# The FFN of a hybrid block: 16 of the 22 inner tiles of the down projection by seven block products, and a bank of its own for the fourth product of the up projection

## The chip, the core and the metric

One core of a Trainium2 chip runs the whole block. TensorE (PE) multiplies, VectorE (DVE), ScalarE (ACT) and GpSimd (POOL) do elementwise work, SyncE (SP) issues the DMAs; each engine works through its instructions in the order in which they were issued, and semaphores tie the engines together. The metric is the device time of one launch, in microseconds. A profiled execution is one further launch.

## The reference, cut to what matters

Sequence 1024, D_MODEL 1024, D_FF 2816, all in float32. The three mixers before the FFN are not touched.

```python
h = rms_norm(x, pre_ffn_norm[l])
u = causal_dwconv(h @ ffn_w_up[l], ffn_conv_w[l], ffn_conv_b[l])   # 1024 x 5632, three taps
gate, val = jnp.split(u, 2, axis=-1)
f = (jax.nn.gelu(gate, approximate=True) * val) @ ffn_w_down[l]    # 2816 -> 1024
x = x + rms_norm(f, post_ffn_norm[l])
```

## The kernel before

Everything is held transposed, features on partitions and tokens along the row, so a tile is 128 features by 512 tokens, and h (0 or 1) names the half of the sequence. Each float32 product is made of three matmuls on operands split into a high and a low part: hi·hi, hi·lo, lo·hi, each 128x128 by 128x512 (all recorded at line L208). ACT makes the high part by a copy into the matmul type; DVE or POOL makes the low part, a subtraction with two inputs in SBUF.

The 2816 inner features are 22 tiles f. Tile f has a gate tile (2f) and a value tile (2f+1) in the up projection.

*Up projection.* The first four f go directly (`up_half`, L1530). The other 18 go through `up_pair` (L1537). It regards gate and value for the two halves of the sequence as a 2x2 block matrix and makes it by seven block products instead of eight. A block product is four steps of 128 inner features with three matmuls each, so 12 matmuls, and one pair costs 84. `weights7` (L500) loads the two weight tiles (`wraw`, three buffers in rotation) and makes the seven weight operands: `whi`/`wlo` (products 1 and 2), `uf` with `uhi`/`ulo` twice (products 3, 6 and 5, 7), `ahi`/`alo` (product 4). ACT makes the high parts, POOL the sums `uf` and the low parts: per pair eight operations at L512 to L526. The activations' combinations are made once, ahead of the loop (L1571 to L1589).

In `up_pair` three PSUM banks x, y, z take the products; a `snap` (L1510) is ACT's copy of a bank into SBUF. Products 1, 6, 5 and 3 accumulate in x, product 2 goes to y, products 7 and 4 accumulate in z. DVE adds the first snap to y (L1545) and takes the second from z (L1557); POOL takes the third from the snap of z (L1555). `conv` applies the three taps: ACT writes the first, DVE adds two (L310), and for h = 1 two short operations add the halo of two columns that h = 0 left (L312). For h = 1 the value tile's conv reads the snap s7, in SBUF. ACT applies gelu (L1524), DVE multiplies gate by value (`gated`, L1527), and SP stores the tile m to `m_d` in DRAM.

*Down projection.* It goes over the inner tiles in chunks, `DOWN`: (first tile, count) = (0,4), (4,4), (8,4), (12,4), (16,2) and, in the tail with the norm, (18,4). `m_split` (L1598) reloads m, ACT makes the high part (L1601), DVE the low part (L1602). `down` (L1608) goes over the eight output tiles j: it loads and splits a weight tile (`load_w`, L267: ACT L272, POOL L273), runs 12 matmuls per tile of four inner tiles for each half, and adds the bank to the accumulator `acc[h][j]` in SBUF (L1617; for the first chunk ACT copies it, L1615). The first chunk's reload stands inside the last up pair (`between`), and all loads are issued by SP in program order; buffers come free when the matmuls that read them are done. What stands after (18,4), the norm and the residual, is the tail, L1634 on.

The banks named `dense` rotate in one pool, `psd`; the tail has another, `psn`.

Of the kernel before, what the change touches and what calls it, by code (L numbers as in the profile page):

```python
# [23 lines left out]
NFF = 22  # L24
# [68 lines left out]
def layout(a):  # L93
# [31 lines left out]
    for i, (c0, c1) in enumerate(TM_CHUNKS):  # L125
# [16 lines left out]

    dns = [units(dn[c * 128:(c + n) * 128], ar(DM)) for c, n in DOWN]
    out.update(
# [9 lines left out]
        wup=units(up, fch), **{f"wdn{i}": d for i, d in enumerate(dns)})  # L154
# [4 lines left out]
DOWN = [(0, 4), (4, 4), (8, 4), (12, 4), (16, 2), (18, 4)]  # L159
# [25 lines left out]
U_BUFS = 4  # L185
OSQ = 6

# [1169 lines left out]
def tail_stage(nc, tc, es, env):  # L1357
# [152 lines left out]
    def snap(ps):  # L1510
        s = up_.tile([128, 512], F32, name="snap", bufs=5)
        act(s, ps, AF.Copy)
# [24 lines left out]
    def up_pair(f, rhs, between=None):  # L1537

        st = {}
        w = E.weights7(wx, A["wup"][2 * f], A["wup"][2 * f + 1], 512)  # L1540
        x, y, z = bank(), bank(), bank()
        E.product(x, w, rhs, 1, True)
        s1 = snap(x)
        E.product(y, w, rhs, 2, True)
        V.tensor_tensor(y, y, s1, op=OP.add)  # L1545
        conv(2 * f, 0, y, st)
        E.product(x, w, rhs, 6, False)
        s2 = snap(x)
# [6 lines left out]
        P.tensor_tensor(s7, s7, s3, op=OP.subtract)  # L1555
        E.product(z, w, rhs, 4, False)
        V.tensor_tensor(z, z, s2, op=OP.subtract)  # L1557
# [14 lines left out]
    later = []  # L1572
    for k in range(4):
        quarters = [(1, h2[0, k]), (2, h2[0, k + 4]), (3, h2[1, k + 4])]
        lows = [rows[0][k], rows[1][k], rows[0][k + 4], rows[1][k + 4]]
        E.combos(*lows, V)
        for q, b in quarters:
            rhs[q][k] = b
        t2, t1, t4, t3 = lows
        for q, t in ((6, t2), (7, t3)):  # L1580
            rhs[q][k] = hi, lo = x_t(), x_t()
            act(hi, t, AF.Copy)
            V.tensor_tensor(lo, t, fl(hi), op=OP.subtract)
        later += [(5, k, t1, hi_t), (4, k, t4, lo_t)]

    for q, k, t, place in sorted(later, key=lambda x: (-x[0], x[1])):
        rhs[q][k] = hi, lo = place(), x_t()
        act(hi, t, AF.Copy)
        V.tensor_tensor(lo, t, fl(hi), op=OP.subtract)  # L1589
# [3 lines left out]
    def m_tile(f, h, s):  # L1593
        t = x_t(F32) if s is None else up_.tile([128, 512], F32, name=f"u{s}")
        nc.sync.dma_start(t, m_d[f * 128:(f + 1) * 128, hs(h)])
        return t

    def m_split(f, h):  # L1598
        src = m_tile(f, h, None if f < DOWN[0][1] else f % 2)
        hi, lo = hi_t(), lo_t()  # L1600
        act(hi, src, AF.Copy)  # L1601
        V.tensor_tensor(lo, src, fl(hi), op=OP.subtract)  # L1602
        return hi, lo
# [4 lines left out]
    def down(ci, f0, nf, ms):  # L1608
        end = None
        for j in range(8):  # L1610
            pss = fm_unit(psd, load_w(A[f"wdn{ci}"][j], nf * 128), lambda k, h: ms[f0 + k, h], nf)
            for h, ps in enumerate(pss):
                a = acc[h][j]
                if ci == 0:
                    act(a, ps, AF.Copy)  # L1615
                else:
                    end = V.tensor_tensor(a, a, ps, op=OP.add)  # L1617
        return end


    ms0 = {}
    for f in range(N_FIRST, NFF):
        up_pair(f, rhs, (lambda: ms0.update(m_chunk(*DOWN[0]))) if f == NFF - 1 else None)

    last = len(DOWN) - 1
    tc.keep_in_program_order(nc.scalar.preload_act_table_set(E.TABLE))
    for ci, (f0, nf) in enumerate(DOWN[:last]):
        if ci == 0:
            acc = [[x_t(F32) for _ in range(8)] for _ in range(2)]
        i = down(ci, f0, nf, m_chunk(f0, nf) if ci else ms0)  # L1630
        if ci == last - 2:
            late = i
# [5 lines left out]
    def w_split(j, place):  # L1638
        ws.append(load_w(A[f"wdn{last}"][j], 512, place, up_.tile([128, 512], F32, name="snap", bufs=5)))
# [17 lines left out]
    def norm_rows(ss, W):  # L1657
# [7 lines left out]
        rb = up_.tile([128, 512], F32, name="u1")  # L1665
# [15 lines left out]
    for s0, s1 in LAST:  # L1681
# [3 lines left out]
        ss = up_.tile([128, 512], F32, name="u0")  # L1685
        for j in range(8):
# [10 lines left out]
            else:  # L1697
                sq = up_.tile([128, 512], F32, name="snap", bufs=5)
# [24 lines left out]
```

## Time and profile before

| what | us |
| --- | --- |
| three runs | 2288.7, 2292.17, 2292.13 |
| their median | 2292.13 |
| the profiled execution | 2297.28 |
| its span | 2295.5 |
| mean granted clock of PE | 0.985 |
| first block product after the last wait at its start | 1699.38 |
| end of the wait at the border of up and down projection | 2011.85 |

In the profile a row of a group names line, engine, operation, output and inputs with their shapes, the count, the busy time and the mean of one, and behind the bar the idle time of the engine just before these instructions and what ended it. A row of the waits gives the engine that waited, what it waited for, and the sum in us, how often and the longest. In a timeline a row gives the start, the duration, and in brackets the idle time before. The clock is the share of the full rate that was granted to PE.

### The profile page before, as it was taken

To read this page: it belongs to the slowest core of one execution; us is meant where nothing else is said; L and a number is where in the kernel's file an instruction comes from. 1 tells how busy PE (TensorE), PEld (TensorE's weight loads), DVE (VectorE), ACT (ScalarE), POOL (GpSimd) and SP (SyncE) were. 2 spreads that over 40 slices of the span, in tenths; PEclk is the share of its full clock that TensorE was granted. 3 is DMA by queue.
4 is the path that set the end of the run, shared out by engine and by line. 5 is a ranking of instruction groups with operands and counts; after the bars stand their busy time and mean duration, and the time that the engine had idled before them with its cause. 6 is when DMAs were issued, how large, how long until landed. Compare 5 with 4: busy or idle time off the path is not lost.

```text
span 2295.5 us, 29758 instructions
## 1 busy us (share of the span) xinstructions
PE 2197.3 (96%) x10663; PEld 1755.3 (76%) x10663; DVE 1346.2 (59%) x2376; ACT 1164.9 (51%) x2185; POOL 1184.5 (52%) x853
## 2 busy tenths in 40 slices
PE   7999999998999999999999999999899999999997
PEld 7878889865665678878775678887678888878886
DVE  7765554268567526556536653359876777744346
ACT  6544443466756646667755421245545555553124
POOL 3676741246736733333347655446578888822213
PEclk9999999999999999999999999999999999999998
DMA  4233341320221011112253253334322222264212
GB/s 170 81 111 108 116 132 62 112 70 24 62 67 31 12 56 42 60 65 93 83 211 112 80 213 129 119 128 162 106 79 86 85 83 83 84 223 130 93 32 74
DMA packets 115349, 222.03 MB, mean 97 GB/s; under 512 B 28160, under 2 KB 42432, under 8 KB 115200
## 3 DMA queue, kind: packets, MB, share of 16 engines
q1 hardware_dynamic: 112608, 217.80, 28.0%
q10 hardware_dynamic: 2592, 2.32, 0.3%
q8 instruction: 84, 1.38, 0.2%
q14 instruction: 65, 0.53, 0.1%
HBM read 162.80 MB, written 57.28 MB: 96 GB/s over the span
## 4 chain that ended last, share of the span: by engine, by line
PE 77%; DVE 11%; ACT 5%; issue 3%; DMA 3%; POOL 2%; SPq 0%; DVEq 0%; ACTq 0%; POOLq 0%
PE dense L208 55%; PE ps_s L208 7%; PE ps_o L208 6%; PE ps_t L208 6%; PE ps_b L208 4%; POOL wlo L273 1%; DVE x L1484 1%; DVE mx L938 1%; DVE u L310 1%; DVE osq L1457 1%; DVE x L1589 1%; DMA wraw<-in_wdn 1%; DMA wraw<-in_wfm 0%; DVE x L1677 0%; DMA x<-in_xT 0%
## 5 line engine op out<-in xcount | busy, mean ns | idle before, releaser
L273 POOL TENSOR_TENSOR wlo<-wraw,whi 128x1024 fp32r<-128x1024 f32 (+2 forms) x134 | 266.5, 1989 | 444.1 <-ACT whi L272 435.4
L208 PE MATMUL dense<-hi,whi 128*128 128x512 f32 x816 | 308.2, 392 | 4.8 <-ACT whi L272 4.8
L208 PE MATMUL dense<-hi,wlo 128*128 128x512 f32 x752 | 289.3, 394 | 8.9 <-POOL wlo L273 7.9
L208 PE MATMUL dense<-lo,whi 128*128 128x512 f32 x688 | 269.3, 392 | 0.5 <-POOL lo L1497 0.5
L208 PE MATMUL dense<-h_hi,whi 128*128 128x512 f32 x656 | 263.8, 402 | 0.0
L208 PE MATMUL dense<-h_lo,whi 128*128 128x512 f32 x656 | 257.5, 393 | 0.0
L208 PE MATMUL dense<-h_hi,wlo 128*128 128x512 f32 x656 | 257.2, 392 | 0.0
L272 ACT ACTIVATE whi<-wraw 128x1024 fp32r<-128x1024 f32 (+2 forms) x134 | 116.1, 867 | 277.4 <-PE dense L208 228.8
L976 POOL TENSOR_TENSOR wT_lo<-wT,wT_hi 128x512 fp32r<-128x512 f32 x132 | 168.5, 1288 | 101.3 <-ACT wT_hi L975 93.2
L208 PEld LDWEIGHTS dense<-hi,whi 128*128 128x128 f32 x816 | 154.2, 189 | 39.5 <-ACT whi L272 6.9
L208 PE MATMUL dense<-x,uhi 128*128 128x512 f32 x552 | 177.3, 392 | 3.9 <-ACT x L584 2.4
L208 PEld LDWEIGHTS dense<-hi,wlo 128*128 128x128 f32 x752 | 142.1, 189 | 41.7 <-POOL wlo L273 10.4
L208 PEld LDWEIGHTS dense<-lo,whi 128*128 128x128 f32 x688 | 130.0, 189 | 28.6 <-POOL lo L1497 1.4
L208 PEld LDWEIGHTS dense<-h_hi,wlo 128*128 128x128 f32 x656 | 123.7, 189 | 26.7
L208 PEld LDWEIGHTS dense<-h_hi,whi 128*128 128x128 f32 x656 | 124.4, 190 | 23.8
L208 PEld LDWEIGHTS dense<-h_lo,whi 128*128 128x128 f32 x656 | 124.3, 189 | 22.5
L1180 POOL TENSOR_TENSOR s_lo<-sa,s_hi 128x512 fp32r<-128x512 f32 (+2 forms) x48 | 53.5, 1115 | 152.1 <-ACT s_hi L1179 152.1
L938 DVE TENSOR_REDUCE mx<-ps_t 128x1 f32<-128x384 f32 (+3 forms) x192 | 98.7, 520 | 47.7 <-PE ps_t L208 44.0
L208 PEld LDWEIGHTS dense<-x,uhi 128*128 128x128 f32 x552 | 103.7, 189 | 27.5 <-ACT x L584 3.6
L965 ACT ACTIVATE wT<-ps_s 128x512 f32<-128x512 f32 x132 | 78.4, 594 | 72.4 <-PE ps_s L208 67.1
L310 DVE SCALAR_TENSOR_TENSOR u<-dense,pv,u 128x510 f32<-128x510 f32 (+1 forms) x140 | 101.9, 737 | 7.8 <-ACT u L306 7.6
L521 POOL TENSOR_TENSOR ulo<-uf,uhi 128x1024 fp32r<-128x1024 f32 x30 | 72.5, 2418 | 63.4 <-ACT uhi L520 63.4
(514 smaller groups left out, 5690.9 us busy)
## 6 DMA issues: line engine op xcount, KB each, us to landing
wraw<-in_wfm SPq DMA_DIRECT2D x62, 512.0 KB, 3.7
wraw<-in_wup SPq DMA_DIRECT2D x52, 512.0 KB, 3.7
g_d<-gate_e SPq DMA_DIRECT2D x48, 256.0 KB, 2.1
s_d<-o SPq DMA_DIRECT2D x48, 256.0 KB, 2.0
ge<-g_d SPq DMA_DIRECT2D x24, 512.0 KB, 3.5
m_d<-u SPq DMA_DIRECT2D x44, 256.0 KB, 2.0
u<-m_d SPq DMA_DIRECT2D x36, 256.0 KB, 4.0
row<-s_d SPq DMA_DIRECT2D x16, 512.0 KB, 4.2
```

Of the source, the lines that this page charges most:

```text
L208: i = f(*a, **k)
L272: act(hi, raw, AF.Copy)
L273: (V if tiles else P).tensor_tensor(lo, raw, fl(hi), op=OP.subtract)
L310: V.scalar_tensor_tensor(o[:, d:], ps[:, :512 - d], taps[d], o[:, d:], op0=OP.mult, op1=OP.add)
L521: P.tensor_tensor(l24, f24, fl(h24), op=OP.subtract)
L938: V.tensor_reduce(mx[:, h, a, n:n + 1], pm[:, :w], axis=AX, op=OP.max)
L965: act(w.rearrange("p h q -> p (h q)"), pz, AF.Exp)
L976: P.tensor_tensor(lo, wf, fl(hi), op=OP.subtract)
L1180: (P if SB_SLO else V).tensor_tensor(s_lo[:, c0:], a[:, c0:], fl(s_hi[:, c0:]), op=OP.subtract)
L1457: eng.tensor_tensor(sums[0], sums[0], sq, op=OP.add)
L1484: e.tensor_tensor(o[j], o[j], x, op=OP.add)
L1589: V.tensor_tensor(lo, t, fl(hi), op=OP.subtract)
```

## The change

Down projection: the inner tiles 4 to 19 go in four chunks of four (`DOWN7`) through `down7`. In a chunk the four inner tiles make two 2x2 block matrices of m (two inner tiles by the two halves of the sequence), k = 0 and 1; an output block takes two steps of 128, and there are two halves d of the output (four tiles each). Each half d takes one `weights7` call on weights stored in the matching order (`wds`), and seven block products for n = 0 and 1, each 2 x 3 matmuls: 84 matmuls for a half, 672 for all. Each product is added to, or taken from, one accumulator tile as its bank is done: 14 evictions for a half. The remaining tiles go as before, (20,2) by `down` and (0,4) in the tail.

The combinations of m are made in the up loop: for every two inner tiles `combine` makes four DVE operations on SBUF tiles, deferred into the following pair, and SP issues 14 stores of a 128x512 tile to a new scratch `m7_d`, where it issued four to `m_d`. `m_sets` reloads them, 14 tiles for a chunk, each with a copy by ACT and a split by DVE; the load goes straight into the tile of the low part. The first chunk's loads stand in the last up pair, as before; chunk c's loads stand in the program ahead of chunk c's products.

Up projection: the fourth product gets a bank v from the pool `psn`. The snap of z and POOL's subtraction go. DVE takes the second snap's place by `s2 = z - s2`, then `v += s2` and `z -= s3`; the conv of h = 1 for the value tile reads the bank z.

Buffers: gate tiles `u0` 6, value tiles `u1` 2, snaps 6 (before: four, four and five).

```diff
-DOWN = [(0, 4), (4, 4), (8, 4), (12, 4), (16, 2), (18, 4)]
+DOWN7 = [4, 8, 12, 16]
+DOWN = [(20, 2), (0, 4)]
...
+U0_BUFS = 6
+U1_BUFS = 2
+SNAPS = 6
 OSQ = 6
...
     m_d = E.scratch("m_d", [NFF * 128, T])
+    m7_d = E.scratch("m7_d", [4 * len(DOWN7) // 2 * 7 * 128, 512])
 
     def conv(u, h, ps, st):
         s = u % 2
         if h == 0:
             st["halo", s] = up_.tile([128, 4], F32, name="halo", bufs=12)
-        st[s, h] = up_.tile([128, 512], F32, name=f"u{s}")
+        st[s, h] = up_.tile([128, 512], F32, name=f"u{s}", bufs=(U0_BUFS, U1_BUFS)[s])
         E.conv(st[s, h], h, ps, [pvc(PV_FW, 3 * u + 2 - d) for d in range(3)], pvc(PV_FB, u), st["halo", s])
         if s == 0:
             act(st[0, h], st[0, h], AF.Gelu_apprx_tanh)
 
+    even = {}
+    def in_pairs(f):
+        return DOWN7[0] <= f < DOWN7[-1] + 4
+    def m7_rows(p, q):
+        r = (7 * p + q - 1) * 128
+        return m7_d[r:r + 128, :]
     def gated(f, h, st):
-        V.tensor_tensor(st[0, h], st[0, h], st[1, h], op=OP.mult)
-        nc.sync.dma_start(m_d[f * 128:(f + 1) * 128, hs(h)], st[0, h])
+        m = st[0, h]
+        V.tensor_tensor(m, m, st[1, h], op=OP.mult)
+        if not in_pairs(f):
+            nc.sync.dma_start(m_d[f * 128:(f + 1) * 128, hs(h)], m)
+            return
+        if f % 2 == 0:
+            even[h] = m
+            q = {0: 1}.get(h)
+        else:
+            q = 2 + h
+        p = (f - DOWN7[0]) // 2
+        if q:
+            nc.sync.dma_start(m7_rows(p, q), m)
+        if f % 2 and h:
+            later.extend(combine(p, even[0], even[1], st[0, 0], m))
+    later = []
+    def combine(p, b11, b12, b21, b22):
+        t7, t6, t4 = [up_.tile([128, 512], F32, name="snap", bufs=SNAPS) for _ in range(3)]
+        def one():
+            V.tensor_tensor(t7, b12, b22, op=OP.subtract)
+            V.tensor_tensor(b12, b11, b12, op=OP.subtract)
+            for q, t in ((7, t7), (5, b12)):
+                nc.sync.dma_start(m7_rows(p, q), t)
+        def two():
+            V.tensor_tensor(t6, t7, b11, op=OP.subtract)
+            V.tensor_tensor(t4, t6, b21, op=OP.add)
+            for q, t in ((6, t6), (4, t4)):
+                nc.sync.dma_start(m7_rows(p, q), t)
+        return one, two
+    def deferred():
+        if later:
+            later.pop(0)()
 
...
         st = {}
         w = E.weights7(wx, A["wup"][2 * f], A["wup"][2 * f + 1], 512)
         x, y, z = bank(), bank(), bank()
+        v = psn.tile([128, 512], F32, name="psn", tag="psn")
         E.product(x, w, rhs, 1, True)
         s1 = snap(x)
         E.product(y, w, rhs, 2, True)
         V.tensor_tensor(y, y, s1, op=OP.add)
         conv(2 * f, 0, y, st)
+        deferred()
         E.product(x, w, rhs, 6, False)
         s2 = snap(x)
         if between:
             between()
         E.product(z, w, rhs, 7, True)
-        s7 = snap(z)
+        V.tensor_tensor(s2, z, s2, op=OP.subtract)
         E.product(x, w, rhs, 5, False)
         s3 = snap(x)
-        P.tensor_tensor(s7, s7, s3, op=OP.subtract)
-        E.product(z, w, rhs, 4, False)
-        V.tensor_tensor(z, z, s2, op=OP.subtract)
-        conv(2 * f + 1, 0, z, st)
+        E.product(v, w, rhs, 4, True)
+        V.tensor_tensor(v, v, s2, op=OP.add)
+        conv(2 * f + 1, 0, v, st)
+        V.tensor_tensor(z, z, s3, op=OP.subtract)
         gated(f, 0, st)
+        deferred()
         E.product(x, w, rhs, 3, False)
-        conv(2 * f + 1, 1, s7, st)
+        conv(2 * f + 1, 1, z, st)
         conv(2 * f, 1, x, st)
         gated(f, 1, st)
 
...
-    def m_tile(f, h, s):
-        t = x_t(F32) if s is None else up_.tile([128, 512], F32, name=f"u{s}")
-        nc.sync.dma_start(t, m_d[f * 128:(f + 1) * 128, hs(h)])
-        return t
+    def split_in(src):
+        hi, lo = hi_t(), lo_t()
+        return split_to(hi, lo, src)
+    def split_to(hi, lo, src):
+        nc.sync.dma_start(fl(lo), src)
+        act(hi, fl(lo), AF.Copy)
+        V.tensor_tensor(lo, fl(lo), fl(hi), op=OP.subtract)
+        return hi, lo
 
     def m_split(f, h):
-        src = m_tile(f, h, None if f < DOWN[0][1] else f % 2)
-        hi, lo = hi_t(), lo_t()
-        act(hi, src, AF.Copy)
-        V.tensor_tensor(lo, src, fl(hi), op=OP.subtract)
-        return hi, lo
+        return split_in(m_d[f * 128:(f + 1) * 128, hs(h)])
+    def m_sets(c):
+        sets = [{}, {}]
+        for n, q in enumerate(ORDER7):
+            for i, st in enumerate(sets):
+                if (2 * c + i) % 3 == 2 and n < 5:
+                    hi, lo = x_t(), x_t()
+                else:
+                    hi, lo = hi_t(), lo_t()
+                st[q] = split_to(hi, lo, m7_rows(2 * c + i, q))
+        return sets
+    def down7(c, sets):
+        def product2(ps, q, n, first):
+            hi, lo = w[q]
+            for k in range(2):
+                s = slice((2 * n + k) * 128, (2 * n + k + 1) * 128)
+                b = sets[k][q]
+                for m, (x, y) in enumerate(((hi, b[0]), (hi, b[1]), (lo, b[0]))):
+                    mm(ps, x[:, s], y, start=first and k == 0 and m == 0, stop=k == 1 and m == 2,
+                       skip_group_check=True)
+        def add(h, j, ps, op, first):
+            a = acc[h][j]
+            if first and c == 0:
+                act(a, ps, AF.Copy, scale=1.0 if op == OP.add else -1.0)
+            else:
+                return V.tensor_tensor(a, a, ps, op=op)
+        end = None
+        for d in range(2):
+            w = E.weights7(wx, A[f"wds{c}"][d, 0], A[f"wds{c}"][d, 1], 512)
+            x, y, z = [[bank(), bank()] for _ in range(3)]
+            if c == 0:
+                for n in range(4):
+                    for h in range(2):
+                        acc[h].append(x_t(F32))
+            for q, ps, start, outs in ((1, x, True, ((0, 0, OP.add, True),)),
+                                       (2, y, True, ((0, 0, OP.add, False),)),
+                                       (6, x, False, ((0, 1, OP.subtract, True),)),
+                                       (7, z, True, ((1, 1, OP.add, True),)),
+                                       (5, x, False, ((1, 1, OP.subtract, False),)),
+                                       (4, z, False, ((0, 1, OP.add, False),)),
+                                       (3, x, False, ((1, 0, OP.add, True),))):
+                for n in range(2):
+                    product2(ps[n], q, n, start)
+                    for h, m, op, first in outs:
+                        end = add(h, 4 * d + 2 * n + m, ps[n], op, first)
+        return end
 
     def down(ci, f0, nf, ms):
-        end = None
         for j in range(8):
             pss = fm_unit(psd, load_w(A[f"wdn{ci}"][j], nf * 128), lambda k, h: ms[f0 + k, h], nf)
             for h, ps in enumerate(pss):
                 a = acc[h][j]
-                if ci == 0:
-                    act(a, ps, AF.Copy)
-                else:
-                    end = V.tensor_tensor(a, a, ps, op=OP.add)
-        return end
-
-
-    ms0 = {}
+                V.tensor_tensor(a, a, ps, op=OP.add)
+    acc = [[], []]
+    sets = []
     for f in range(N_FIRST, NFF):
-        up_pair(f, rhs, (lambda: ms0.update(m_chunk(*DOWN[0]))) if f == NFF - 1 else None)
-
+        up_pair(f, rhs, (lambda: sets.extend(m_sets(0))) if f == NFF - 1 else None)
+    tc.keep_in_program_order(nc.scalar.preload_act_table_set(E.TABLE))
+    for c in range(len(DOWN7)):
+        if c:
+            sets = m_sets(c)
+        late = down7(c, sets)
     last = len(DOWN) - 1
-    tc.keep_in_program_order(nc.scalar.preload_act_table_set(E.TABLE))
     for ci, (f0, nf) in enumerate(DOWN[:last]):
-        if ci == 0:
-            acc = [[x_t(F32) for _ in range(8)] for _ in range(2)]
-        i = down(ci, f0, nf, m_chunk(f0, nf) if ci else ms0)
-        if ci == last - 2:
-            late = i
+        down(ci, f0, nf, m_chunk(f0, nf))
 
...
```

More of the change, by code (lines that the diff above doesn't have):

```diff
@@ L143, in layout @@
     dns = [units(dn[c * 128:(c + n) * 128], ar(DM)) for c, n in DOWN]
+    dns7 = [np.ascontiguousarray(dn[c * 128:(c + 4) * 128].reshape(2, 2, 128, 2, 2, 2, 128)
+                                 .transpose(3, 5, 2, 1, 4, 0, 6).reshape(2, 2, 128, 1024)) for c in DOWN7]
     out.update(
@@ L1510, in snap @@
     def snap(ps):
-        s = up_.tile([128, 512], F32, name="snap", bufs=5)
+        s = up_.tile([128, 512], F32, name="snap", bufs=SNAPS)
         act(s, ps, AF.Copy)
@@ L1571, in tail_stage @@
     rhs = {q: [None] * 4 for q in range(1, 8)}
-    later = []
+    parts = []
     for k in range(4):
@@ L1583, in tail_stage @@
             V.tensor_tensor(lo, t, fl(hi), op=OP.subtract)
-        later += [(5, k, t1, hi_t), (4, k, t4, lo_t)]
-    for q, k, t, place in sorted(later, key=lambda x: (-x[0], x[1])):
+        parts += [(5, k, t1, hi_t), (4, k, t4, lo_t)]
+    for q, k, t, place in sorted(parts, key=lambda x: (-x[0], x[1])):
         rhs[q][k] = hi, lo = place(), x_t()
@@ L1638, in w_split @@
     def w_split(j, place):
-        ws.append(load_w(A[f"wdn{last}"][j], 512, place, up_.tile([128, 512], F32, name="snap", bufs=5)))
+        ws.append(load_w(A[f"wdn{last}"][j], 512, place, up_.tile([128, 512], F32, name="snap", bufs=SNAPS)))
     for k in range(nf):
@@ L1664, in norm_rows @@
         E.rsqrt_mean(rt[:, :n], v[:, :n], ps[:, :n], DM)
-        rb = up_.tile([128, 512], F32, name="u1")
+        rb = up_.tile([128, 512], F32, name="u1", bufs=U1_BUFS)
         act(rb[:, :W].rearrange("p (n t) -> p n t", t=128), rt[:, :n, None].to_broadcast([128, n, 128]), AF.Copy)
@@ L1684, in tail_stage @@
         W = s1 - s0
-        ss = up_.tile([128, 512], F32, name="u0")
+        ss = up_.tile([128, 512], F32, name="u0", bufs=U0_BUFS)
         for j in range(8):
@@ L1697, in tail_stage @@
             else:
-                sq = up_.tile([128, 512], F32, name="snap", bufs=5)
+                sq = up_.tile([128, 512], F32, name="snap", bufs=SNAPS)
                 act(sq[:, :W], a, AF.Square)
```

4 lines of the change are left out of this document (3 added, 1 removed).

## The prediction

> **What bounds the kernel now.** I read the totals first, then the stretches in which the change lies, then in each the chain and the waits of PE.
>
> ```profile
> span 2295.5 us, 29758 instructions
> PE 2197.3 (96%) x10663; PEld 1755.3 (76%) x10663; DVE 1346.2 (59%) x2376; ACT 1164.9 (51%) x2185; POOL 1184.5 (52%) x853
> ```
>
> PE is busy for 96% of the span. The busy time by stretch (engine: busy us, instructions; then clock and DMA) shows the two stages: the up projection by block products to about 2010, the down projection to about 2260.
>
> ```profile
> 1700.00:1800.00 100.00, 100.00 (x436) 82.44 (x435) 67.16 (x90) 50.61 (x72) 84.88 (x50) 0.99 0.24 82
> 1900.00:2000.00 100.00, 100.00 (x443) 82.81 (x442) 71.62 (x95) 53.31 (x77) 83.53 (x47) 1.00 0.24 82
> 2000.00:2100.00 100.00, 94.52 (x407) 77.11 (x406) 49.83 (x77) 45.62 (x77) 31.58 (x22) 0.98 0.57 195
> 2100.00:2200.00 100.00, 100.00 (x443) 82.80 (x442) 36.25 (x53) 21.12 (x35) 24.01 (x19) 1.00 0.24 78
> ```
>
> In both stages PE is full and starts 443 matmuls in 100 us: 0.226 us each. The 392 ns that the page gives as the mean of one would be wrong here, since neighbours overlap. One up pair (84 matmuls) is 19.0 us. POOL is at 84% in the up stage, 24% in the down stage; DVE at 70% and 36%. The chain in the up stage is one piece of PE:
>
> ```profile
> 1699.38 280.64 PE dense L208 x1229
> ```
>
> So matmuls saved are time saved, as long as POOL and DVE, which get the new work, don't become the bound. From 1700 on PE waits little:
>
> ```profile
> PE psn L208 <- ACT u L1666: 6.8, 2, 4.3
> PE dense L208 <- ACT snap L1512: 5.1, 2, 3.0
> PE dense L208 <- ACT whi L272: 2.3, 1, 2.3
> ```
>
> The 6.8 lie in the tail, which stays. The other two contain the border between the stages, where ACT's snap stands behind the hi copies that wait for the reloaded m:
>
> ```profile
> 2008.42 0.39 PE L208 MATMUL dense<-hi,wlo 128*128 128x512 f32 x1
> 2011.85 0.50 PE L208 MATMUL dense<-lo,ahi 128*128 128x512 f32 x1 [3.04 <-ACT snap L1512]
> ...
> 2013.34 0.59 PE L208 MATMUL dense<-lo,ahi 128*128 128x512 f32 x1
> ...
> 2016.71 0.43 PE L208 MATMUL dense<-hi,ulo 128*128 128x512 f32 x1
> ```
>
> After the wait eight matmuls take 3.37 us instead of 1.8: a stall of 3.0 costs 1.6 more in clock. The border costs 3.0 + 1.6 + 2.3 = 6.9 us.
>
> **The change part by part.**
>
> *A, matmuls.* 16 inner tiles cost 768 matmuls before, and 4 chunks × 2 halves × 84 = 672 after. 96 × 0.226 = **−21.7 us**, certain as long as PE is the bound.
>
> *B, up stage: the fourth product in its own bank.* It removes one ACT snap per pair and POOL's subtraction; DVE gets three PSUM adds instead of two, and the conv of h=1 reads PSUM instead of SBUF.
>
> ```profile
> L1555 POOL TENSOR_TENSOR snap<-snap 128x512 f32<-128x512 f32 x16 | 20.7, 1294 | 0.0
> L521 POOL TENSOR_TENSOR ulo<-uf,uhi 128x1024 fp32r<-128x1024 f32 x16 | 38.4, 2400 | 27.7 <-ACT uhi L520 27.7
> L520 ACT ACTIVATE uhi<-uf 128x1024 fp32r<-128x1024 f32 x16 | 17.0, 1060 | 30.4 <-PE dense L208 24.1 <-POOL uf L519 6.3
> L525 ACT ACTIVATE ahi<-wraw 128x512 fp32r<-128x512 f32 x16 | 10.1, 632 | 18.8 <-PE dense L208 18.8
> wraw<-in_wup SPq DMA_DIRECT2D x52, 512.0 KB, 3.7
> L310 DVE SCALAR_TENSOR_TENSOR u<-snap,pv,u 128x510 f32<-128x510 f32 x16 | 44.8, 2797 | 0.0
> L310 DVE SCALAR_TENSOR_TENSOR u<-dense,pv,u 128x510 f32<-128x510 f32 x46 | 33.8, 735 | 0.0
> L1557 DVE TENSOR_TENSOR dense<-dense,snap 128x512 f32<-128x512 f32 x16 | 11.2, 699 | 11.3 <-PE dense L208 11.3
> ```
>
> POOL falls from 83.5% of 19.0 = 15.9 to 14.6 us a pair. DVE loses 2.1 on the conv and gains 0.7 for the add and, per pair, two subtractions with two SBUF inputs for the block combinations of m (0.7 each if free, 2.8 each if held like the 2797 row): 13.6 becomes 13.6 … 17.8 of 19.0. By itself none of these binds.
>
> What speaks against it is order. The fourth product no longer shares the bank z, and in the order that the changed program issues it runs for the next pair ahead of this pair's seventh. So the next pair's ahi copy stands on ACT ahead of this pair's remaining work (the copy uhi24 that POOL's ulo needs, the snap that the third product needs), and it waits for a wraw load that SP issues only when POOL's last read of the buffer is done. The loop that results is POOL 14.6 + load 3.7 + ahi 0.63 + uhi 1.06 = 20.0 us against 19.0 for PE: 1.0 late. It closes in two of three pairs, as three wraw buffers rotate, in about 15 pairs from the sixth inner tile on. In the third the load goes out earlier by an ulo and more (some 2.5 us), which wins back up to 1.5. So each three pairs lose between 0.5 and 2.0, five times: 2.5 to 10. I take **+6 us**. The bounds: 0 where POOL, less disturbed, needs its undisturbed sum 3 × 2.40 + 5 × 1.30 = 13.7 (loop 19.1; the 1.30 is a row below), and 15 × 2.4 = +36 where POOL is held as long as before (15.9, loop 21.3) in every pair. A gain is excluded: PE had no wait there.
>
> The stores of m7, 14 per two inner tiles instead of 4, add 10 × 0.25 MB in 38 us: 69 GB/s to the 82 of the row, where 195 stands in the row at 2000. Cost 0, unless a store that waits for a late DVE subtraction holds the wraw load behind it on SP; that goes into the same upper bound.
>
> *C, border.* The next stage's first operands now come as splits of which all but the last were stored long before, and the last up pair has the fourth product's bank. But weights7 puts whi, ahi and two uhi on ACT where one whi stood. I take 2 us of the 6.9 as left, **−5 us** (bounds −7 and 0).
>
> *D, second chunk.* Each chunk of the down projection loads 14 m7 tiles.
>
> ```profile
> u<-m_d SPq DMA_DIRECT2D x36, 256.0 KB, 4.0
> L1601 ACT ACTIVATE hi<-u 128x512 fp32r<-128x512 f32 x36 | 21.3, 627 | 5.8 <-DMA u<-m_d 2.9 <-PE dense L208 2.4
> L1602 DVE TENSOR_TENSOR lo<-u,hi 128x512 fp32r<-128x512 f32 x36 | 25.1, 737 | 27.6 <-ACT hi L1601 27.6
> L1602 DVE TENSOR_TENSOR lo<-x,hi 128x512 fp32r<-128x512 f32 x8 | 7.7, 988 | 3.0 <-ACT hi L1601 3.0
> L1617 DVE TENSOR_TENSOR x<-x,dense 128x512 f32<-128x512 f32 x64 | 43.9, 687 | 86.6 <-PE dense L208 86.5
> L1589 DVE TENSOR_TENSOR x<-x,lo x4: 1772/2866/2880, 1683.3 to 1690.6; 128x512 fp32r<-128x512 f32 x4
> ```
>
> In the issued order SP has chunk 1's first operand (its buffer long free) behind prefetch loads of chunk 2 whose buffers are freed by the last products of chunk 0. PE then waits for load 4.0 + hi 0.63 + lo 0.74 to 2.87: 5.4 to 7.5 us, with up to 1.6 of slow clock; bounds 0 (buffers free early) and 9. I take **+6**. The later chunks have their first operands in time.
>
> *E, DVE in the down stage.* Per half chunk (19.0 us) it has 7 splits and 12 adds. The adds take 12 × 0.687 = 8.2. The splits have two SBUF inputs, and those wait for POOL here. In the rows below, four splits beside POOL took 6.88 and four more (the L1589 row) up to 2.88 each, and POOL's 2.40 became 2.92:
>
> ```profile
> 1676.53 6.88 DVE L1589 TENSOR_TENSOR x<-x,hi 128x512 fp32r<-128x512 f32 x4
> 1675.28 1.30 POOL L522 TENSOR_TENSOR uf<-wraw 128x512 f32<-128x512 f32 x1
> 1676.54 2.92 POOL L512 TENSOR_TENSOR wlo<-wraw,whi 128x1024 fp32r<-128x1024 f32 x1
> ```
>
> POOL goes from 24% to 13.7 of 19.0, 72%. At 0.74 a split DVE is at 13.4 us per half; at 2.87 at 28.3. It becomes the bound above (19.0 − 8.2) / 7 = 1.54 a split. Met at random, an operation waits for what is left of POOL's: (3 × 2.40² + 5 × 1.30²) / (2 × 19.0) = 0.68, so 1.4 a split, an estimate from these rows: 18.0 us, 95%. It fits on average and bunches: **+4 us**. Bounds 0, and 2.0 a split (8.2 + 14.0 = 22.2, 3.2 late in each of 7 halves) +22; all at 2.87 would be far beyond, but the adds read PSUM and let POOL's operations pass meanwhile. POOL itself has 13.7 and up to 3 of being held: below 19.0.
>
> Beside these rows stands the Trainium skill, SBUF — State Buffer, section "SBUF: two separate sides": GpSimd and a DVE operation with two SBUF inputs take the shared port pair as an exclusive lock, the later one fully blocks. By that rule a backlogged DVE alternates with POOL, 0.69 + 1.7 a split, as the 2.87 beside 2.92 bears out; with 2.4 a split it would be E's bad case, +42. The sum does not use it.
>
> Sum against the profiled 2297.28: −21.7 + 6 − 5 + 6 + 4 = **−10.7**, to 2286.6. That run lay 0.22% above the median of the runs, 2292.13; less 0.47% the forecast is **2281 us**.
>
> **The rivals.**
>
> *1, everything is covered.* B, D and E at 0 to 2, the border gone: −21.7 − 7 + 3 = −26, 2266 us. For it: POOL gets lighter, and each new wait sits by less than 1.1 us. Against: the late load of D is in the issued order. Chance 0.22.
>
> *2, the weights loop becomes the bound of the up stage (slower).* Place: ACT's ahi ahead of uhi24 and snap; price: POOL stays at 15.9 because DVE's new subtractions hold it, loop 21.3 each pair, 15 × 2.4 = 36. It decides above 1.8 us a pair (27 us, which eats the other −17). With the rest as forecast −21.7 + 36 − 5 + 6 + 4 = +19: 2311 us. For it: the 2797 row, the L1589 rows. Against: before, POOL had idle time in every pair (27.7 us over 16 before L521), and a late loop spreads POOL's work. Chance 0.20.
>
> *3, DVE bounds the down stage (slower).* At 2.0 a split: −21.7 + 6 − 5 + 6 + 22 = +7, 2299 us; it decides from 1.9 on. Against: splits may run 14 products ahead, and the 0.988 row was with POOL at 24%. Chance 0.15.
>
> *4, nothing to measure:* B and E each somewhat over, +11 more, 2292 us. Chance 0.06.
>
> **How the numbers follow.** The forecast has 0.37 (its own range 2274 to 2287: B 2.5 to 10, E 0 to 6). Rivals 0.22, 0.20, 0.15, 0.06. A measurement here can tell about 0.2%, ±4.6 us, from no change. Faster 0.37 + 0.22 = 0.59, same 0.06, slower 0.35. The range that leaves out a tenth on each side reaches from rival 1's 2266 (a little under, for −7 and the border at once: 2263) to rival 2's 2311.
>
> **What would show it.** A: 672 matmuls in the middle of the down stage at 0.226. B: waits of PE for ACT's snap or uhi of about 1 us in two of three pairs, ACT's idle time put down to the wraw load, POOL under 80%; wrong if PE stays one piece. C: the wait at the border below 3. D: one wait of 5 to 8 us some 38 us into the down stage, released by a split whose load landed late. E: the mean split 1.2 to 1.6, DVE over 85%, PE waiting for a lo in the first three chunks; wrong if the mean is below 1. Wrong altogether: more than one slow stretch of the clock in the up stage, or PE waiting for a free bank.

## The result, and the profile after

The changed kernel takes 2342.49 us (median of 4 runs, 2340.41 to 2347.62), the kernel before 2290.41 in the same comparison: a ratio of 1.0234, interval 1.022 to 1.0249. The change makes the kernel 52 us slower, where 2281 was forecast. The profiled execution took 2340.41 us. The page's totals of the kernel after:

```profile
span 2338.7 us, 29794 instructions
PE 2191.4 (94%) x10567; PEld 1739.5 (74%) x10567; DVE 1502.6 (64%) x2516; ACT 1175.1 (50%) x2191; POOL 1227.9 (53%) x867
```

The 96 matmuls are gone (10567 against 10663), and PE is busy for a smaller share of a longer span. The busy time by stretch shows where:

```profile
1700.00:1800.00 100.00, 91.85 (x394) 74.34 (x393) 81.40 (x103) 42.77 (x62) 67.73 (x38) 0.98 0.24 82
1900.00:2000.00 100.00, 91.53 (x379) 74.35 (x378) 81.12 (x102) 38.65 (x56) 64.71 (x38) 0.93 0.23 82
2000.00:2100.00 100.00, 85.55 (x351) 68.40 (x350) 84.01 (x105) 48.15 (x73) 60.12 (x32) 0.93 0.43 150
2100.00:2200.00 100.00, 86.68 (x360) 68.04 (x359) 80.18 (x88) 42.84 (x65) 67.14 (x37) 0.95 0.42 140
```

The up stage, where PE was full, starts 379 to 394 matmuls in 100 us instead of 436 to 443. POOL, which had 84%, is now at 65 to 68%: it does less and waits more. The down stage is as broken, at 0.93 to 0.95 of the clock. PE's waits from 1660 on (in total, times, longest):

```profile
PE dense L219 <- ACT snap L1523: 29.4, 15, 4.8
PE dense L219 <- DVE u L321: 8.4, 2, 6.7
PE dense L219 <- DVE x L1696: 6.5, 7, 1.7
...
PE psn L219 <- DVE x L1651: 5.5, 4, 1.8
PE dense L219 <- ACT x L1662: 4.5, 1, 4.5
PE dense L219 <- DVE x L1663: 3.4, 1, 3.4
```

29.4 us stand behind ACT's snap (15 times). In eleven of the last fifteen up pairs PE waits for it for 1.2 us or more, in the other four not at all at that place. One pair with such a wait, put together in order of time from the timelines of POOL, SP, ACT and PE (start, duration, engine, line; in brackets the idle time before and its releaser):

```profile
1864.33 1.30 POOL L530 TENSOR_TENSOR uf<-uf,wraw 128x512 f32<-128x512 f32 x1
1866.20 0.33 SPq L1561 DMA_DIRECT2D m_d<-u  x1
1866.93 0.32 SPq L1575 DMA_DIRECT2D m_d<-snap  x1
...
1868.34 0.38 SPq L517 DMA_DIRECT2D wraw<-in_wup  x1
1871.68 0.63 ACT L536 ACTIVATE ahi<-wraw 128x512 fp32r<-128x512 f32 x1 [5.26 <-DMA wraw<-in_wup]
1872.22 0.76 ACT L317 ACTIVATE u<-psn,pv 128x512 f32<-128x512 f32 x1
1872.88 1.04 ACT L531 ACTIVATE uhi<-uf 128x1024 fp32r<-128x1024 f32 x1
1873.82 1.07 ACT L1523 ACTIVATE snap<-dense 128x512 f32<-128x512 f32 x2
1874.00 2.69 POOL L532 TENSOR_TENSOR ulo<-uf,uhi 128x1024 fp32r<-128x1024 f32 x1 [8.37 <-ACT uhi L531]
1874.46 0.50 PE L219 MATMUL dense<-hi,uhi 128*128 128x512 f32 x1 [2.23 <-ACT snap L1523]
```

Read it downwards. POOL has read the weight buffer for the last time at 1865.6. SP issues the load that ahi needs only at 1868.3, behind a store of m and a store of a combination that wait for DVE. The load lands at 1871.7, and ACT has stood still for it for 5.26 us, since the next pair's ahi stands first in its queue. Only then come the bank of the fourth product, the uhi for which POOL has waited 8.4 us, and the snap for which PE waits.

The totals contain a wobble: the first store of m starts between 1593 and 1603 us in the profiled executions, though next to nothing ahead of it was edited, and the runs of the kernel before alone spread from 2284.8 to 2296.1 (17 runs, beside e9). So I compare the stretch from there to the end of the span, "FFN" below: 2295.5 − 1603.1 = 692.4 before, 2338.7 − 1593.7 = 745.0 after, +52.6.

```profile
L1528 SPq DMA_DIRECT2D m_d<-u x44: 319/326/812, 1603.1 to 2050.7; - x44
```

```profile
L1552 SPq DMA_DIRECT2D m_d<-u x12: 319/324/327, 1593.7 to 2093.3; - x12
```

(Busy ns least, median, most, then the first and the last start, of before and of after.)

### The profile page after: what moved, and what is told of

Its sections match the earlier page's. It is cut to its first block, busy times and chain, and to the rows that moved or that the text cites. A ratio compares the mean times of both kernels' runs of the same rounds, so it can differ in the third digit from the quotient of the medians.

```text
span 2338.7 us, 29794 instructions
## 1 busy us (share of the span) xinstructions
PE 2191.4 (94%) x10567; PEld 1739.5 (74%) x10567; DVE 1502.6 (64%) x2516; ACT 1175.1 (50%) x2191; POOL 1227.9 (53%) x867
## 4 chain that ended last, share of the span: by engine, by line
PE 67%; DVE 15%; ACT 6%; issue 5%; DMA 4%; POOL 3%; SPq 0%; DVEq 0%; ACTq 0%; POOLq 0%
PE dense L219 44%; PE ps_s L219 7%; PE ps_o L219 6%; PE ps_t L219 6%; PE ps_b L219 4%; DVE u L321 2%; DVE u L323 2%; DMA wraw<-in_wup 1%; PE psn L219 1%; DVE lo L1663 1%; DMA lo<-m_d 1%; DVE u L1550 1%; DVE mx L949 1%; POOL wlo L284 1%; DVE x L1495 1%
## 5 line engine op out<-in xcount | busy, mean ns | idle before, releaser
L284 POOL TENSOR_TENSOR wlo<-wraw,whi 128x1024 fp32r<-128x1024 f32 (+2 forms) x102 | 223.5, 2192 | 323.3 <-ACT whi L283 308.3
L219 PE MATMUL dense<-hi,whi 128*128 128x512 f32 x608 | 228.8, 395 | 13.6 <-DVE u L321 8.4
L219 PE MATMUL dense<-hi,wlo 128*128 128x512 f32 x544 | 213.8, 398 | 8.5 <-POOL wlo L284 8.1
L219 PE MATMUL dense<-x,uhi 128*128 128x512 f32 x600 | 193.4, 394 | 2.4 <-ACT x L595 2.4
L219 PE MATMUL dense<-lo,whi 128*128 128x512 f32 x480 | 189.5, 395 | 0.7 <-POOL lo L1508 0.5
L532 POOL TENSOR_TENSOR ulo<-uf,uhi 128x1024 fp32r<-128x1024 f32 x38 | 93.3, 2457 | 179.9 <-ACT uhi L531 179.9
L283 ACT ACTIVATE whi<-wraw 128x1024 fp32r<-128x1024 f32 (+2 forms) x102 | 95.8, 940 | 170.2 <-PE dense L219 134.8
L219 PEld LDWEIGHTS dense<-hi,whi 128*128 128x128 f32 x608 | 115.8, 190 | 41.9 <-DVE u L321 9.2
L219 PE MATMUL dense<-hi,uhi 128*128 128x512 f32 x248 | 103.2, 416 | 34.9 <-ACT snap L1523 29.4
L219 PEld LDWEIGHTS dense<-hi,wlo 128*128 128x128 f32 x544 | 103.5, 190 | 33.1 <-POOL wlo L284 10.1
L535 POOL TENSOR_TENSOR ulo<-uf,uhi 128x1024 fp32r<-128x1024 f32 x38 | 92.1, 2424 | 34.8 <-ACT uhi L534 32.3
```

Source lines behind the costliest of these rows:

```text
L219: i = f(*a, **k)
L283: act(hi, raw, AF.Copy)
L284: (V if tiles else P).tensor_tensor(lo, raw, fl(hi), op=OP.subtract)
L532: P.tensor_tensor(l24, f24, fl(h24), op=OP.subtract)
L535: P.tensor_tensor(l31, f31, fl(h31), op=OP.subtract)
```

## The experiments

e1 to e4 and e10 are single runs, the others medians of 10 or 12; FFN is from the one profiled execution of each.

| run | what it is | us | FFN us |
| --- | --- | --- | --- |
| before | | 2285 to 2291, by comparison | 692.4 |
| after | | 2342.5 | 745.0 |
| e1 | before, with only the fourth product's bank | 2335.3 | 730.8 |
| e2 | after, with the old up pair | 2294.0 | 697.1 |
| e3 | after, fourth product kept behind the fifth | 2290.9 | 695.1 |
| e4 | e1 with a fourth weight buffer | 2292.2 | 688.4 |
| e5 | e3, early loads for the second chunk | 2289.3 | 691.1 |
| e6 | e5, first chunk's loads behind the third snap | 2295.5 | 695.2 |
| e7 | e5, last stores of m behind those loads | 2290.9 | 691.2 |
| e8 | e7, first chunk's loads in two parts | 2290.3 | 692.0 |
| e9 | e7, bank copies ahead of operand copies | 2289.0 | 690.0 |
| e10 | e9, half of the weights left out | 2277.8 | 679.9 |

**e1, e2, e3: which part, and by its order or by its load.** e1 puts the new bank into the kernel before, e2 takes it out of the changed kernel, e3 leaves everything in and fixes one order:

```diff
-        E.product(x, w, rhs, 5, False)
+        i = E.product(x, w, rhs, 5, False)
         s3 = snap(x)
-        E.product(v, w, rhs, 4, True)
+        with tc.issue_after(i.ins):
+            E.product(v, w, rhs, 4, True)
```

> The kernel before with only the up projection's edit: the fourth product in a bank of its own, down projection as before, no combinations of m and no stores of them. Theory A (order): the fourth product of the next pair is issued ahead of this pair's seventh, so the next ahi copy stands on ScalarE ahead of the uhi copy and of the snap that the third product waits for; this alone makes PE wait for the snap, 0.5 us or more a pair on the mean, total 2300 to 2320. Rival B (load): it is the four subtractions of m on VectorE and the 14 stores ahead of the weight loads on SyncE that make the pair late; without them no wait for the snap, total 2280 to 2292.

> The changed kernel with the up projection's pair as before (fourth product in the bank of the seventh, GpSimd's subtraction back); combinations, stores and the down projection by block products stay. Theory A: the waits for the snap in the up stage go (29 us of wait and some 8 us of slow clock), total 2300 to 2310. Rival B: they stay, total 2330 to 2345, or longer, as GpSimd has 1.3 us more a pair.

> The changed kernel, whole, with one order added: the fourth product's matmuls are issued behind the fifth's last one, so that they can't run a pair ahead. Theory A: as in the run with the old pair, waits for the snap under 5 us over the stage, total 2300 to 2310. Rival B: the waits stay, total 2330 to 2345.

The kernel before took 2289.58 us beside them. e1, which has neither combinations nor the new down projection, takes 2335.28: the bank alone costs 38 us of the FFN. Its waits and its POOL:

```profile
PE dense L208 <- ACT snap L1512: 27.6, 16, 3.4
```

```profile
L521 POOL TENSOR_TENSOR ulo<-uf,uhi 128x1024 fp32r<-128x1024 f32 x16 | 38.3, 2393 | 116.6 <-ACT uhi L520 109.5 <-PE dense L208 7.2
```

So the waits need no combination of m: theory B falls. In e3 the combinations, the stores and a DVE at 86% are all there, and PE is full again in the up stage:

```profile
1700.00:1800.00 100.00, 100.00 (x442) 82.53 (x441) 86.29 (x117) 49.80 (x70) 74.11 (x42) 1.00 0.30 98
2000.00:2100.00 100.00, 86.56 (x340) 68.36 (x339) 79.42 (x98) 52.73 (x80) 63.59 (x34) 0.90 0.47 164
2100.00:2200.00 100.00, 96.15 (x418) 77.75 (x417) 83.74 (x105) 36.67 (x54) 64.66 (x36) 1.00 0.41 127
```

One ordering edge takes back 50 of the 52.6 us of the FFN (745.0 to 695.1). (e1 was expected at 2300 to 2320 and cost more; e2 and e3 came 6 to 9 us below what was expected, and e3's waits for the snap are 8.0 us, where under 5 was expected.) But e3 has 96 matmuls fewer and is no faster than before: the border and the down stage give them back, from 2000 on.

**e4: what closes the loop.** The fourth product still runs a pair ahead; the weights get a fourth buffer (and the snaps four instead of five, for its room):

```diff
-            raw = (wx if turn[0] % 3 == 2 else wp).tile([128, 1024], F32, name="wraw", bufs=1 + (turn[0] % 3 < 2))[:, :2 * n]
+            other = turn[0] % rot[0] >= 2
+            raw = (wx if other else wp).tile([128, 1024], F32, name="wraw", bufs=rot[0] - 2 if other else 2)[:, :2 * n]
```

> The kernel before with the fourth product in its own bank (the first run again, 2335 us), with a fourth buffer for the loaded weights, so that a pair's load needs no longer wait for the last read of the pair just ahead, and four snaps instead of five; the fourth product still runs a pair ahead. Theory A1: what closes the loop is the load (GpSimd's last read, SyncE's issue, the load's 3.5 us, then the ahi copy); with the load a pair earlier the waits for the snap are under 5 us over the stage and the total is 2285 to 2298. Rival A2: the place of ahi on ScalarE alone, with the engines' chain behind it, makes the pair late, whenever the load lands: total 2320 to 2337.

e4 took 2292.19 us. Its waits, and the up stage:

```profile
PE dense L208 <- ACT snap L1515: 0.3, 1, 0.3
```

```profile
1900.00:2000.00 100.00, 100.00 (x443) 82.84 (x442) 81.89 (x106) 50.08 (x70) 75.03 (x43) 1.00 0.23 76
```

27.6 us of waits became 0.3 with the same order on ACT. So ahi's place is harmless as long as its load is there, and it is the load that closes the loop: A1 holds, A2 falls.

**e5 to e8: the late operands of the down stage.** In e3 PE waits 4.7 us for the second chunk's first operand. Its load goes out at 2071.6, behind 29 loads of other operands, of which the first two chunks need only 23: the rest are for later ones. Its buffer comes from the pool of the accumulators and has long been free (in e9 the same load goes out at 1791.5). My reading is that the program grants the slots of a pool in its own order, so that this one stands behind the accumulators of the first chunk; that is argued, not shown apart from the place in SP's queue. e5 places these five loads ahead of the second half's accumulators (the rest of the edit passes them on to the second chunk):

```diff
         for d in range(2):
+            if c == 0 and d == 1:
+                m_ahead(1)
```

> The changed kernel with the fourth product kept behind the fifth (2290.9 us) and, in addition, the five loads of the second chunk whose buffers are free since the up projection placed ahead of the accumulators that the second half of the first chunk takes from the same pool. Theory C: the wait at the second chunk (4.7 and 1.5 us, and slow clock behind it) is a load issued late; it goes, total 2278 to 2285. Rival D: VectorE with splits of 1.3 us is the bound there; PE then waits as long for splits a few products later, total 2288 to 2293.

> As the run before it, and the first chunk's loads and copies are issued behind the last pair's third snap instead of behind its second. If the wait of 3.3 us at the border is ScalarE's snap behind copies that wait for their loads, it goes with its slow clock, and the total is 3 to 7 us below the run before it; if the first products of the down projection then wait for those loads instead, it is the same or up to 5 us above.

e5 took 2289.28, ratio to before 1.0003 (0.9988 to 1.0019); e6 2295.46, 1.0027 (1.0015 to 1.0038). In e5 the wait at the chunk's start is gone, and a longer one stands in the chunk before it: ACT's copy of a bank, due since 2058, behind operand copies that wait for later loads.

```profile
2062.21 0.63 ACT L1664 ACTIVATE hi<-lo 128x512 fp32r<-128x512 f32 x1 [0.83 <-DMA lo<-m_d]
2062.80 1.27 ACT L1664 ACTIVATE x<-x 128x512 fp32r<-128x512 f32 x2
2063.98 1.06 ACT L1707 ACTIVATE x<-dense 128x512 f32<-128x512 f32 x2
2064.61 0.80 PE L219 MATMUL dense<-hi,uhi 128*128 128x512 f32 x1 [6.49 <-ACT x L1707]
```

The total lies in D's range, but neither C nor D holds as put: the stall moved to another queue. e6 came 6.2 us above e5, more than the 5 that its worse case allowed. The wait at the border went from ACT to DVE, where nine splits (15.7 us) now stood ahead of the conv, and grew to 12.6 us:

```profile
2036.90 0.76 PE L219 MATMUL dense<-hi,uhi 128*128 128x512 f32 x1 [12.58 <-DVE u L323]
```

e7 issues the last inner tile's two stores, for which SP was held 8.4 us in e5, behind the early loads; e8 leaves only four of the first chunk's loads at their old place.

```diff
+                with tc.issue_after(loaded[0].ins):
+                    for store in held:
+                        store()
```

> The run with the early loads (2289.3 us) with one more order: the two stores of the last inner tile's m, which SyncE otherwise holds for 8.4 us until VectorE has made it, are issued behind the second chunk's early loads. Theory C2: in that run PE's wait of 6.5 us in the first chunk (ScalarE's copy of a bank behind copies that wait for late loads) comes from SyncE being held there; the loads land some 10 us earlier, the wait falls under 2 us, total 2279 to 2285. Rival D: the loads then wait as long for their buffers or for GpSimd's reads of the weights, which stand on the same queue; the wait stays, total 2287 to 2291.

> As the run before it, and of the first chunk's 14 loads and copies only the first four stand in the last pair behind its second snap; the other ten come behind the value tile's conv. If PE's wait of 4.0 us at the border is ScalarE's snap behind the fifth to eighth copy, whose loads come late, it falls under 1 us and with it the slow clock behind it: 4 to 7 us below the run before it. If the ten late copies make VectorE's splits late for the first products, PE waits there instead and nothing is won.

e7 took 2290.92 (ratio 1.0013, 1.0003 to 1.0023) and e8 2290.27 (1.0006, 0.9994 to 1.0019): nothing is won. In e7 SP was free of the stores, and the loads stood nearly as long behind the next thing in its queue, the weights' load, which waits until POOL has read the buffer, at 2046.2. Theory C2 falls, and rival D had it:

```profile
2044.42 1.74 POOL L530 TENSOR_TENSOR uf<-uf,wraw 128x512 f32<-128x512 f32 x1
2046.18 0.33 SPq L517 DMA_DIRECT2D wraw<-in_wds  x1
2046.57 0.42 SPq L1670 DMA_DIRECT2D x<-m_d  x1
2063.68 0.80 PE L219 MATMUL dense<-hi,uhi 128*128 128x512 f32 x1 [7.29 <-ACT x L1714]
```

In e8 both waits were as before (3.79 and 7.88 us).

**e9: the queues as they should be.** The early loads stand ahead of all accumulators of their pool, and the second chunk's other copies behind ACT's bank copies:

```diff
+        if c == 1:
+            with tc.issue_after(copies[13].ins):
+                sets = m_sets(c)
```

> The run with the stores behind (2290.9 us), with the second chunk's five early loads placed ahead of all accumulators of their pool, and the copies of that chunk's other operands behind ScalarE's bank copies of the first chunk. Theory C3: PE's wait of 7.3 us in the first chunk is ScalarE's in-order queue, a bank copy behind operand copies whose loads are late; the wait falls under 3 us and the slow clock behind it goes, total 2280 to 2285, below both kernels. Rival D: the operands that now are copied later make VectorE's splits late and PE waits as long at the second chunk's start; total 2288 to 2293.

e9 took 2289.00, ratio 0.9991 (0.9978 to 1.0004). The wait of 7.3 us is gone, and PE waits for DVE instead:

```profile
PE dense L219 <- DVE x L1721: 9.8, 9, 3.3
```

```profile
L1674 DVE TENSOR_TENSOR lo<-lo,hi 128x512 fp32r<-128x512 f32 x50 | 59.7, 1211 | 11.9 <-ACT hi L1673 11.9
```

C3 was right in its mechanism and wrong in the total; rival D, with its total, describes what took its place.

**e10: half of GpSimd's work.** The second half of each chunk multiplies by the first half's weights.

```diff
-            w = E.weights7(wx, A[f"wds{c}"][d, 0], A[f"wds{c}"][d, 1], 512)
+            if d == 0:
+                w = E.weights7(wx, A[f"wds{c}"][d, 0], A[f"wds{c}"][d, 1], 512)
```

> The run with the banks first, with the weights of a chunk's second half left out (the second half multiplies by the first half's weights, so GpSimd, ScalarE and SyncE prepare half as many in the down projection; the matmuls and evictions are all there). Theory E: in the down stage VectorE's splits (1.3 us instead of 0.74) and PE's waits for bank evictions (9.8 us) come from GpSimd's work on the weights; with half of it the mean split is 0.95 to 1.1 and those waits are under 5 us. Rival F: they come from the number of splits and evictions alone, 28 us of them in each 38; the mean split falls but the waits stay at 8 us or more.

e10 took 2277.83, with 2285.02 for the kernel before beside it.

```profile
PE dense L219 <- DVE x L1721: 1.8, 3, 1.0
```

```profile
L1674 DVE TENSOR_TENSOR lo<-lo,hi 128x512 fp32r<-128x512 f32 x46 | 43.6, 967 | 12.3 <-ACT hi L1673 12.2
```

```profile
2090.00:2128.00 38.00, 38.00 (x170) 31.45 (x169) 31.90 (x43) 12.57 (x18) 14.94 (x8) 1.00 0.32 94
2128.00:2166.00 38.00, 38.00 (x170) 31.45 (x168) 27.88 (x41) 11.07 (x17) 6.85 (x4) 1.00 0.29 87
```

The number of splits and evictions in the stage is the same (the rows count 50 and 46 because their window cuts), POOL's work there falls from 117.5 us in e9 to 56.1, the mean split from 1.21 to 0.97 us, the waits for evictions from 9.8 to 1.8, and PE is full through two chunks. Both forecasts of theory E came true, and rival F falls: the weights' preparation makes DVE late in the down stage. The run takes work from SP and ACT as well as from POOL. That POOL is what stretches the splits is argued from their duration; how much of the shorter waits, and of the 10 us that the FFN gains on e9, is due to SP and ACT was not taken apart.

## Why the prediction was wrong, point by point

*A, the matmuls: right.* PE had 96 fewer, at the same rate wherever nothing waits: 170 in 38 us is 0.2235 each, the 0.226 of the sum within the 1% that missing records and the edges make.

*B, the up stage: the step that failed, in its size.* The mechanism is the one that was named: the fourth product runs a pair ahead, ahi stands ahead of uhi24 and of the snap, and the loop closes through POOL's last read, SP, the load and ACT. It was priced at 20.0 us a pair, late in two of three pairs, won back in the third, and taken at +6. It costs 38 us by itself (e1). e1's sixteen waits for the snap stand at the same place of sixteen pairs in a row. The first and the last are 15 pairs apart, 21.8 us each, 2.8 above PE's 19.0:

```profile
1712.83 0.50 PE L208 MATMUL dense<-hi,uhi 128*128 128x512 f32 x1 [0.34 <-ACT snap L1512]
...
2039.88 0.50 PE L208 MATMUL dense<-hi,uhi 128*128 128x512 f32 x1 [1.32 <-ACT snap L1512]
```

The term that was mis-sized is the latency between POOL's last read and its next work. The forecast has 5.4 us (load 3.7, ahi 0.63, uhi 1.06); it measures 7.7 on the mean of these 15 pairs, for three reasons. In nine of the pairs SP issues the second load not when POOL is done but 1.45 us later, behind a store that waits for DVE: 0.9 on the mean. Both weight loads go out together, and ahi starts 4.5 us after the second issue. And the conv of the fourth bank stands between ahi and uhi (0.6; from 1872.22 to 1872.88 in the pair shown above). The first two in e1's timelines, where POOL is done at 1922.07 (the first row spans two stores; the second of them starts at 1922.65, and the second load at 1923.54):

```profile
1911.01 11.97 SPq L1528 DMA_DIRECT2D m_d<-u  x2
1923.08 0.86 SPq L506 DMA_DIRECT2D wraw<-in_wup  x2
1928.34 0.63 ACT L525 ACTIVATE ahi<-wraw 128x512 fp32r<-128x512 f32 x1 [6.24 <-DMA wraw<-in_wup]
```

In e1 the credit for the third pair fell with that: two loads that leave together have no early one. In the changed kernel every second pair has an early load. There the second load leaves when POOL is done, and POOL pauses for 4.4 to 6.0 us. In the pairs between, the second load leaves 2.5 to 3.0 us late, behind the store of a combination that waits for DVE, and POOL pauses for 7.7 to 10.7. The forecast had named that store, at cost 0 and only in its upper bound. Together it comes to the same: from the place of the wait in the second pair to that in the last, 16 pairs take 346.2 us in e1 and in the changed kernel alike, 21.6 each, and 16 × 2.6 = 42 us more than at PE's pace. In the changed kernel:

```profile
1703.79 0.50 PE L219 MATMUL dense<-hi,uhi 128*128 128x512 f32 x1 [0.34 <-ACT snap L1523]
...
2049.99 0.50 PE L219 MATMUL dense<-hi,uhi 128*128 128x512 f32 x1 [2.63 <-ACT snap L1523]
```

POOL's relief was there, and larger than forecast (it is busy for 207.7 us in e1's 15 pairs, 13.8 each; forecast 14.6). It was of no use, since POOL sat in the loop and waited. So the second rival had the place, and its price of +36 is near the 42, but by luck: it put the lateness down to POOL at 15.9, held by DVE, where POOL worked less and the latency around it was longer.

*C, the border: wrong in sign.* 2 us were to be left of 6.9 (of which the 2.3 do not belong to the border: that wait ends at 2062.27, 50 us behind the other). The last pair waits 2.63 and the first product of the down stage 6.66, for a bank that the conv still reads, because DVE has the first chunk's splits queued ahead of it. PE's timeline and two rows of the chain of waits:

```profile
2065.82 0.80 PE L219 MATMUL dense<-hi,whi 128*128 128x512 f32 x1 [6.66 <-DVE u L321]
```

```profile
2057.84 2.79 DVE lo L1663
...
2061.24 2.73 DVE lo L1663 x2
```

The forecast looked for what might stand ahead on ACT alone. With the fourth product kept in place (e3) the 6.66 are gone, but ACT's snap is waited for as long as before, 3.30 us.

*D, the second chunk: right in its place and its cause, too low in its price.* PE waits 4.5 + 3.4 = 7.9 us, where 5.4 to 7.5 were worked out, and the clock is down behind it:

```profile
2120.00:2140.00 20.00, 12.24 (x42) 9.49 (x43) 16.27 (x16) 6.66 (x10) 11.48 (x6) 0.74 0.43 144
```

The 42 matmuls are 9.5 us at 0.226, so with the waits some 2.6 of the 20 us are slow clock: 10.5 together, above the bound of 9. In SP's queue 30 loads stand ahead of this operand's, seven of them for later chunks, as the forecast had it, and e5 shows that the wait goes with the late load. That its removal gains nothing, as ACT's queue then makes PE wait 6.5 us in the chunk before, the forecast didn't see.

*E, DVE in the down stage: right in its number, too low in its price.* The mean split was put at 1.4 us by chance meeting, and measures

```profile
L1663 DVE TENSOR_TENSOR lo<-lo,hi 128x512 fp32r<-128x512 f32 x44 | 57.9, 1344 | 8.3 <-ACT hi L1662 8.3
```

1.34 in the changed kernel, though POOL is busy for 57% of the stage (113.9 of 199.3 us) and not for 72%. The price of the bunches, +4, measures 6.5 us of waits (L1696). That the waits of C and D are longer too, because DVE works off its queue at that rate, is argued, not shown. By the Trainium skill, SBUF — State Buffer, "SBUF: two separate sides", of a GpSimd operation and a DVE operation with two SBUF inputs the later one blocks fully. The trace agrees: of the 68 splits at L1663, 33 take 0.7 us and the longest takes 2.89, so the mean lies between free and fully blocked.

*The sum.* The two traces differ by exactly the 96 matmuls, so the FFN can be cut at equal counts of matmuls:

| stretch, and its matmuls | before us | after us | difference |
| --- | --- | --- | --- |
| first store of m to the first pair | 74.3 | 74.2 | −0.1 |
| to the place of the wait in the second pair, 108 | 32.0 | 35.9 | +3.9 |
| 16 pairs, 1344 | 309.6 | 346.2 | +36.6 |
| rest of the last pair and the border, 60 | 13.6 | 25.2 | +11.6 |
| down projection to the tail, 864 before, 768 after | 198.9 | 199.3 | +0.4 |
| tail | 64.0 | 64.2 | +0.2 |

The 16 pairs before contain their wait of 3.0 us at the border, with its slow clock. The +3.9 come with the fourth product too: in the first pair it runs ahead to where its operands aren't ready (5.5 us, L1651; 5.4 in e1). In the down projection the 21.7 us of the 96 matmuls are lost again: PE waits for 18.2 us where it waited for 2.4, and the rest is slow clock. So against the forecast's −21.7 + 6 − 5 + 6 + 4 stand −21.7, some +40 and +12 in the up projection and at the border, and +22 in the down projection. The loop of B is the largest error. With it out of the way (e3) the FFN is still 2.7 us longer than before, where the forecast without B's +6 would be 16.7 shorter: that is the share of C, D and E. The range stopped at 2311, where only the largest of these terms came true.

*Which version is best:* e9, e5 and e8 are level with the kernel before; none beats it clearly. e4, without the new down projection, has an FFN 4 us shorter than before, in a single run. e10 is not a candidate, as it leaves out weights. What less GpSimd work in the down stage would gain with the right weights, and e4's fourth weight buffer beside the new down projection, was not tried.

## What to carry to other kernels

A bank of its own removes a dependence, and with it an order that held other things in place: look in the order as issued for what now runs ahead, and follow what it drags to the head of each in-order queue. A loop that passes through a queue is as long as the queue's other waits, so add up what stands ahead of each of its links, not only the links; if one more buffer or one ordering edge opens it, the price can be 50 us for one line. And matmuls taken from a stage that PE bounds are worth their time only if the operands that replace them come in time; here they were made by DVE while POOL prepared the weights, and DVE's splits took nearly twice as long.

## What the runs showed of the hardware

The stretch ahead of the FFN differs by up to 10 us between the profiled executions, so a difference of a few microseconds is better read from the stage's own start. The clock did not follow the length of a wait. Two rows of the kernel before: after a wait of 2.01 us the next matmul takes 0.80, and the granted clock is 0.72 in the 5 us from 1700 on; after one of 2.28 us it takes 0.50, and the clock is 1.00 from 2060 to 2070. After the 3.04 us at the border six matmuls follow at full pace, and the slow ones begin 1.5 us behind the wait, at 2013.34.

```profile
1699.38 0.80 PE L208 MATMUL dense<-hi,uhi 128*128 128x512 f32 x1 [2.01 <-ACT snap L1512]
...
2062.27 0.50 PE L208 MATMUL dense<-hi,whi 128*128 128x512 f32 x1 [2.28 <-ACT whi L272]
```
